# One VectorE scaling per attention step, one head's value sum on GpSimd, the outputs' split one step later, and output products spread over steps 10 to 15

## The chip, the core and the metric

The kernel runs on one core of a Trainium2 chip. The core has five engines that work side by side: TensorE (PE in the profile; its weight loads are PEld), VectorE (DVE), ScalarE (ACT), GpSimd (POOL) and SyncE (SP), which here only issues DMAs. The metric is the device time of one execution in microseconds (us). Three runs of the kernel before gave 1141.34, 1141.52 and 1141.9 us; the median is 1141.52.

## The reference

A two-layer decoder trunk over 512 tokens of width 1024. Layer 0 mixes tokens by chunked spatial gating, layer 1 by sliding-window attention; each is followed by a gated feed-forward block with a causal convolution and by a gated per-layer embedding. The change lies in the attention of layer 1, which is cut here to what is computed:

```python
q = (xn @ w_q).reshape(B, nb, BLOCK, N_KV_HEADS, GQA_GROUP, HEAD_DIM)      # 4 blocks of 128, 4 groups of 4 heads
scores = jnp.einsum('bnikgd,bnjkd->bnkgij', q, kblk) * (HEAD_DIM ** -0.5)  # previous and own block
scores = scores - slopes * dist;  scores = jnp.where(valid, scores, -jnp.inf)
m = jnp.maximum(jnp.max(scores, axis=-1, keepdims=True), sink)
e = jnp.exp(scores - m)
probs = e / (jnp.sum(e, axis=-1, keepdims=True) + jnp.exp(sink - m))
out = jnp.einsum('bnkgij,bnjkd->bnikgd', probs, vblk)
h = h + out.reshape(B, S, N_Q_HEADS * HEAD_DIM) @ w_o
```

A window of 128 keys over blocks of 128 means that each query has exactly one valid key at each of 128 places, either in its own block or in the one before.

## The kernel before

Activations are kept transposed: eight tiles of 128 features by 512 tokens. To keep float32 precision, each operand of a product is split into a high and a low half (`split`: ScalarE casts the high half, VectorE subtracts to get the low one), and a product is three matmuls: high by high, low by high, high by low (`mm3`, lines 181 to 183). Weights come by DMA into raw tiles (`load`, line 129, on SP's queue), are split in units of 1024 columns (`pump`, lines 154 and 155; four units are held) and are handed out by `chunk`. `more` splits one unit ahead of its use. `pieces` lists the weights in the order of their loads.

The attention runs as 16 steps, one per pair of a group g (four heads) and a block n of 128 queries. Step i does:

- `scores(i)`: eight score matmuls into two PSUM tiles (`sc`), for each head by the high and low half of the keys; VectorE picks for each place the own or the previous block's key (line 784), then adds the distance term and finds the minimum (line 788); ScalarE takes the exponential and its sum (line 793). The result `pr` has two buffers. GpSimd puts the sink into an extra column (line 774).
- `weights(i)`: VectorE takes the reciprocal of the four sums (line 801); the four heads' probabilities are scaled one by one, the first by VectorE (line 807), the other three by ScalarE (line 805).
- `turn(i)`: four transposes by TensorE into one PSUM tile (`tr`, line 822), then a split into halves (lines 252 and 253). For n > 0 GpSimd makes masked copies `u` of both halves (line 830).
- `mix(i)`: two or four matmuls with the values (`pv`, line 844) into one PSUM tile whose upper 64 rows are the contribution of the values' low halves. ScalarE copies those rows down (line 848, `side`), VectorE adds them for one head of each pair at a time (line 852, two instructions). Then the sums are split into the outputs' halves: ScalarE casts `oh` (line 856), GpSimd subtracts for `ol` (line 857), two instructions each.

In the program, step i holds `scores(i)`, other products (`fill(i)`), `mix(i - 2)`, `turn(i - 1)` and `weights(i)`. The parts `scores`, `turn` and `weights` stand under `tc.high_priority()`. The order of instructions on each engine is made by the framework's planner: it takes the instructions whose operands it reckons to be ready by priority, and the priority is the place in the program, with the high-priority ones ahead. An engine then works its queue strictly in order, and waits at an instruction whose operands are late.

`fill(i)` takes its work from the table `beside`. Steps 0 to 9 hold the query projections of the next groups (`project`, twelve matmuls a step from step 2 on), and from step 10 on the output product. `merge(m, k0, k1)` adds for output tile m the slices k0 to k1 of its eight, three matmuls each (L181 to L183 with the name `o`); slices 2g and 2g + 1 need the outputs of group g for all four blocks. A tile m keeps its PSUM bank from its first slice to its last. Slices that are not done in the loop are done behind it, followed by the residual's addition (line 885) and the next norm.

PSUM has eight banks, and every tile of it here takes one. The single raw weight tile that the loop uses (`state["tags"] = [0]`) holds one piece of 2048 columns at a time.

Of the kernel before, what the change touches and what calls it, by code (L numbers as in the profile page):

```python
# [13 lines left out]
P = 128  # L14
# [34 lines left out]
def tile_yoco(ctx: ExitStack, tc: tile.TileContext, t, out: bass.AP, out_b: bass.AP):  # L49
# [58 lines left out]
    plan_cols(t["w_kv"][1:2], 1, KD)  # L108
    plan_cols(t["w_q"][1:4], 3, KD)
    plan_cols(t["w_o"], 4, KD)  # L110
    plan_ffn(1)
# [7 lines left out]
    raws, ready = {}, {}  # L119
    state = {"raw": 0, "unit": 0, "next": 0, "tags": [0, 1, 2], "turn": 0, "pt": 0}  # L120

    def load(upto, queue=nc.sync):
        while state["raw"] < min(upto, len(pieces)):
            j = state["raw"]
            a, m = pieces[j][:2]
            tags = state["tags"]
            r = wp.tile([P, 2 * UNIT], F32, tag=f"r{tags[state['turn'] % len(tags)]}", bufs=1, name=f"wraw{j}")
            state["turn"] += 1
            queue.dma_start(r[:, :m].rearrange("p (c m) -> p c m", c=2) if j in paired else r[:, :m], a)
            raws[j] = r  # L130
            state["raw"] += 1
# [119 lines left out]
    def split(src, hi, lo):  # L251
        nc.scalar.copy(hi, src)  # L252
        nc.vector.tensor_sub(lo, src, hi.bitcast(F32))

    def xtiles(pool, pre, tags):
# [385 lines left out]
    def queries(ps, g, j):  # L641
# [17 lines left out]
        for e, q in enumerate(res):  # L659
            me, it = sides[e], sides[1 - e]  # L660
            nc.sync.dma_start(q[me, :].bitcast(F32), hi[me, :])
            nc.sync.dma_start(q[it, :].bitcast(F32), qf[me, :])
        return res
# [65 lines left out]
    def more():  # L729
# [67 lines left out]
    def weights(i):  # L797

        pr, sm = live[i]
        ds = at.tile([P, GQ], F32, tag="ds", bufs=2, name=f"ds{i}")  # L800
        nc.vector.reciprocal(ds, sm)
        for e in range(GQ):
            a, r = pr[:, e, :P], ds[:, e : e + 1]
            if e:
                nc.scalar.activation(a, a, AF.Copy, scale=r)
            else:
                nc.vector.tensor_scalar_mul(a, a, r)
        live[i] = pr
# [7 lines left out]
    def turn(i):  # L816
# [6 lines left out]
        ph, pl = pair(f"p{i}")  # L823
        split(tr, ph, pl)
        live[i] = [(ph, pl)]
# [9 lines left out]
    def mix(i):  # L835
# [14 lines left out]
        a, low = (x.rearrange("p (b e t) -> p e b t", b=2, e=2) for x in (ps[sides[0], :], low))  # L850
        for e in range(2):
            nc.vector.tensor_add(o[sides[e]], a[:, e], low[:, e])
        cols = slice(n * P, (n + 1) * P)
        for b in range(2):
            oh, ol = o2[2 * g + b]
            nc.scalar.copy(oh[:, cols], o[:, b, :])
            (nc.vector if i == last - 1 else nc.gpsimd).tensor_sub(ol[:, cols], o[:, b, :], oh[:, cols].bitcast(F32))
# [252 lines left out]
```

## Time and profile before

| | us |
|---|---|
| median of three runs | 1141.52 |
| the profiled execution's own time | 1141.22 |
| its span, first to last instruction | 1139.5 |
| PE busy | 1127.0 |
| DVE busy | 749.6 |
| ACT busy | 530.0 |
| POOL busy | 107.7 |

A row of instructions gives: line, engine, operation, out<-in by the program's names, shapes, the count; then busy us, mean ns of one, and the idle time before with what ended it. A row of the order of time begins with start and duration in us, and ends, where the engine idled, with how long and for whom. A row of waits reads: engine and line that waited <- what released it: us in total, times, longest. Matmuls are pipelined, so one is shown for longer than the distance to the start of the next.

### The profile page before, as it was taken

The numbers are of one execution on the slowest core, as the hardware profiler recorded it, in microseconds if no ns is written. First come the engines' busy times: TensorE is split into PE (matmuls) and PEld (weight loads), VectorE is DVE, ScalarE is ACT, GpSimd is POOL, SyncE is SP. The second block draws the span as 40 slices with busy tenths as digits, with TensorE's granted clock in tenths as the row PEclk, the third lists the DMA queues.
The fourth block names the chain that finished last, engine by engine and source line by source line (L and its number), as shares of the span: only waits on it lengthen the run. The fifth ranks groups of instructions, "written<-read, shape, count | busy, mean of one in ns | idle before, by whom it ended". The sixth has DMA issues, their size and how long they took to land.

```text
span 1139.5 us, 13604 instructions
## 1 busy us (share of the span) xinstructions
PE 1127.0 (99%) x5266; PEld 940.5 (83%) x5266; DVE 749.6 (66%) x1158; ACT 530.0 (47%) x875; POOL 107.7 (9%) x175
## 2 busy tenths in 40 slices
PE   9999999999999999999999999999999999999997
PEld 7888888888888888888898878888888888888896
DVE  7366477763677367557988977777636763675675
ACT  6533344441344234445657985444313432355562
POOL 2000200000000000021213343000000000000222
PEclk9999999999999999999999999999999999999999
DMA  8422323223223322432224315223223233224302
GB/s 298 145 83 74 111 75 111 101 85 111 78 98 102 111 76 86 134 107 79 74 75 129 93 38 185 98 88 111 78 107 110 66 102 111 93 80 160 111 1 75
DMA packets 25776, 115.41 MB, mean 101 GB/s; under 512 B 2920, under 2 KB 8176, under 8 KB 16240
## 3 DMA queue, kind: packets, MB, share of 16 engines
q1 hardware_dynamic: 25152, 113.89, 29.8%
q8 instruction: 41, 0.67, 0.2%
q10 hardware_dynamic: 560, 0.66, 0.2%
q14 instruction: 23, 0.19, 0.1%
HBM read 108.24 MB, written 2.11 MB: 97 GB/s over the span
## 4 chain that ended last, share of the span: by engine, by line
PE 95%; DVE 2%; issue 1%; ACT 1%; DMA 1%; POOL 0%; SPq 0%; POOLq 0%; DVEq 0%; ACTq 0%
PE up L181 14%; PE up L183 14%; PE up L182 14%; PE d L183 8%; PE d L181 8%; PE d L182 8%; PE gate L181 2%; PE gate L183 2%; PE gate L182 2%; PE u L182 1%; PE u L183 1%; PE u L181 1%; PE o L182 1%; PE o L181 1%; PE o L183 1%; PE q L181 1%
## 5 line engine op out<-in xcount | busy, mean ns | idle before, releaser
L154 ACT CAST wh<-wraw 128x1024 fp32r<-128x1024 f32 (+2 forms) x197 | 202.0, 1028 | 264.6 <-PE d L182 131.0
L155 DVE TENSOR_TENSOR wl<-wraw,wh 128x1024 fp32r<-128x1024 f32 (+1 forms) x198 | 238.4, 1205 | 127.9 <-ACT wh L154 127.6
L181 PE MATMUL up<-nf00h,wh 128*128 128x512 f32 x352 | 137.1, 390 | 0.0
L181 PE MATMUL up<-nf10h,wh 128*128 128x512 f32 x352 | 137.0, 389 | 0.0
L182 PE MATMUL up<-nf00l,wh 128*128 128x512 f32 x352 | 136.9, 389 | 0.0
L183 PE MATMUL up<-nf00h,wl 128*128 128x512 f32 x352 | 136.9, 389 | 0.0
L183 PE MATMUL up<-nf10h,wl 128*128 128x512 f32 x352 | 136.9, 389 | 0.0
L182 PE MATMUL up<-nf10l,wh 128*128 128x512 f32 x352 | 136.9, 389 | 0.0
L181 PE MATMUL d<-ah,wh 128*128 128x512 f32 x352 | 136.9, 389 | 0.0
L182 PE MATMUL d<-al,wh 128*128 128x512 f32 x352 | 136.9, 389 | 0.0
L183 PE MATMUL d<-ah,wl 128*128 128x512 f32 x352 | 136.9, 389 | 0.0
L379 ACT ACTIVATE c<-hs,vec 128x512 f32<-128x512 f32 x88 | 71.5, 815 | 72.0 <-DVE hs L375 71.2
L380 DVE SCALAR_TENSOR_TENSOR c<-hs,vec,c 128x511 f32<-128x511 f32 x88 | 65.8, 749 | 34.5 <-ACT c L379 34.4
L355 DVE TENSOR_TENSOR h<-h,d 128x512 f32<-128x512 f32 x56 | 38.4, 686 | 73.8 <-PE d L183 73.8
L252 ACT CAST ah<-a 128x512 fp32r<-128x512 f32 x44 | 27.4, 622 | 109.5 <-DVE a L385 109.4
L183 PEld LDWEIGHTS up<-nf10h,wl 128*128 128x128 f32 x352 | 66.1, 188 | 13.8
L182 PEld LDWEIGHTS d<-al,wh 128*128 128x128 f32 x352 | 66.1, 188 | 13.8
L183 PEld LDWEIGHTS up<-nf00h,wl 128*128 128x128 f32 x352 | 66.1, 188 | 13.8
L183 PEld LDWEIGHTS d<-ah,wl 128*128 128x128 f32 x352 | 66.1, 188 | 13.7
L182 PEld LDWEIGHTS up<-nf00l,wh 128*128 128x128 f32 x352 | 66.1, 188 | 13.7
L182 PEld LDWEIGHTS up<-nf10l,wh 128*128 128x128 f32 x352 | 66.1, 188 | 13.7
L181 PEld LDWEIGHTS d<-ah,wh 128*128 128x128 f32 x352 | 66.1, 188 | 13.6
(454 smaller groups left out, 2061.7 us busy)
## 6 DMA issues: line engine op xcount, KB each, us to landing
wraw<-in_w_up SPq DMA_DIRECT2D x44, 1024.0 KB, 4.8
wraw<-in_w_down SPq DMA_DIRECT2D x16, 896.0 KB, 4.6
wraw<-in_w_down SPq DMA_DIRECT2D x8, 1024.0 KB, 4.8
wraw<-in_w_gate SPq DMA_DIRECT2D x8, 1024.0 KB, 4.8
wraw<-in_w_u SPq DMA_DIRECT2D x4, 1024.0 KB, 5.9
wraw<-in_w_out SPq DMA_DIRECT2D x4, 1024.0 KB, 4.8
wraw<-in_w_q SPq DMA_DIRECT2D x4, 1024.0 KB, 4.9
wraw<-in_w_o SPq DMA_DIRECT2D x4, 1024.0 KB, 4.9
```

Source lines behind the costliest of these rows:

```text
L154: nc.scalar.copy(hi, src)
L155: nc.vector.tensor_sub(low, src, hi.bitcast(F32))
L181: nc.tensor.matmul(ps, wh[:, a:b], xh, start=st, stop=False)
L182: nc.tensor.matmul(ps, wh[:, a:b], xl, start=False, stop=False)
L183: nc.tensor.matmul(ps, wl[:, a:b], xh, start=False, stop=en)
L252: nc.scalar.copy(hi, src)
L355: nc.vector.tensor_add(h[m], h[m], ps)
L379: nc.scalar.activation(c, hs, AF.Identity, bias=v("conv_b", l * 2 * NJ + col), scale=cw[2])
L380: nc.vector.scalar_tensor_tensor(c[:, 1:], hs[:, : S - 1], cw[1], c[:, 1:], op0=ALU.mult, op1=ALU.add)
```

## The change

- `weights`: the four scalings become one VectorE product of the 128x4x128 probabilities with the reciprocals, broadcast along the last dimension.
- `mix`: ScalarE copies the first head's rows of `pv` (lower 64 rows, 256 columns) into the tile `side` as well; GpSimd adds the first head's two parts from there; VectorE adds the second head's.
- The split of the outputs becomes a function of its own, `finish`. Up to step 13 `finish(i - 3)` follows `turn(i - 1)`, so an output is split a step later than before; from step 14 on it stands ahead of `fill(i)`. The last two outputs are split right behind their `mix`. For the first eleven an order edge (no wait) puts the cast `oh` behind the latest `split` of transposes on ScalarE.
- The table `beside` has the output products of steps 10 to 17 in another order: four tiles m are begun in steps 10 and 11 with the slices of group 0, those of group 1 follow in steps 12 to 14, those of group 2 in steps 14 and 15. Step 12 has a `more`.
- `queries` and `load`: an order edge puts the load of an output weight piece behind the copies of the queries of one group on SP's queue.

```diff
 def load(upto, queue=nc.sync):
...
-            queue.dma_start(r[:, :m].rearrange("p (c m) -> p c m", c=2) if j in paired else r[:, :m], a)
+            ins = queue.dma_start(r[:, :m].rearrange("p (c m) -> p c m", c=2) if j in paired else r[:, :m], a)
+            for front in state["sent"].pop(j, []):
+                behind(ins, front)
...
 def queries(ps, g, j):
...
+            if g > 1 and j:
+                state["sent"].setdefault(outs + g - 1, []).extend(sent)
...
-        10: [(merge, 0, 0, 3), (more,)],
-        11: [(merge, 0, 3, 4), (merge, 1, 0, 2), (more,)],
-        12: [(merge, 1, 2, 4), (merge, 2, 0, 1)],
-        13: [(merge, 2, 1, 4)],
-        14: [(merge, 0, 4, 6), (merge, 1, 4, 6)],
-        15: [(merge, 2, 4, 6)],
-        16: [(merge, 3, 0, 6)],
-        17: [(merge, 4, 0, 6)],
+        10: [(merge, 0, 0, 2), (merge, 1, 0, 2), (more,)],
+        11: [(merge, 2, 0, 2), (merge, 3, 0, 2), (more,)],
+        12: [(merge, 0, 2, 4), (merge, 1, 2, 4), (more,)],
+        13: [(merge, 2, 2, 4), (merge, 3, 2, 3)],
+        14: [(merge, 3, 3, 4), (merge, 0, 4, 6), (merge, 1, 4, 6)],
+        15: [(merge, 2, 4, 6), (merge, 3, 4, 6)],
+        16: [(merge, 4, 0, 6)],
+        17: [(merge, 5, 0, 6)],
...
 def weights(i):
-        for e in range(GQ):
-            a, r = pr[:, e, :P], ds[:, e : e + 1]
-            if e:
-                nc.scalar.activation(a, a, AF.Copy, scale=r)
-            else:
-                nc.vector.tensor_scalar_mul(a, a, r)
+        a = pr[:, :, :P]
+        nc.vector.tensor_mul(a, a, ds.rearrange("p (e o) -> p e o", o=1).to_broadcast([P, GQ, P]))
...
 def mix(i):
...
-        for e in range(2):
-            nc.vector.tensor_add(o[sides[e]], a[:, e], low[:, e])
+        own_a = side[sides[0], 3 * S + i % 2 * N : 3 * S + (i % 2 + 1) * N].rearrange("p (b t) -> p b t", b=2)
+        nc.scalar.copy(own_a, a[:, 0])
+        nc.vector.tensor_add(o[sides[1]], a[:, 1], low[:, 1])
+        nc.gpsimd.tensor_add(o[sides[0]], own_a, low[:, 0])
+        live[i] = o
+
+    def finish(i):
+        g, n = steps[i]
+        o = live.pop(i)
         cols = slice(n * P, (n + 1) * P)
         for b in range(2):
             oh, ol = o2[2 * g + b]
-            nc.scalar.copy(oh[:, cols], o[:, b, :])
+            ins = nc.scalar.copy(oh[:, cols], o[:, b, :])
+            if i + 3 < LATE:
+                behind(ins, state["split"])
             (nc.vector if i == last - 1 else nc.gpsimd).tensor_sub(ol[:, cols], o[:, b, :], oh[:, cols].bitcast(F32))
...
+    LATE = last - 2
...
+        if LATE <= i < last + 1:
+            finish(i - 3)
         if i <= last:
             fill(i)
         if i >= 2:
             mix(i - 2)
+        if i - 2 >= last - 2:
+            finish(i - 2)
...
+        if 3 <= i < LATE:
+            finish(i - 3)
```

More of the change, by code (lines that the diff above doesn't have):

```diff
@@ L109, in tile_yoco @@
     plan_cols(t["w_q"][1:4], 3, KD)
+    outs = len(pieces)
     plan_cols(t["w_o"], 4, KD)
@@ L119, in tile_yoco, with behind @@
     raws, ready = {}, {}
-    state = {"raw": 0, "unit": 0, "next": 0, "tags": [0, 1, 2], "turn": 0, "pt": 0}
+    state = {"raw": 0, "unit": 0, "next": 0, "tags": [0, 1, 2], "turn": 0, "pt": 0, "split": None, "sent": {}}
+    def behind(ins, front):
+        tc.add_manual_dep(ins.ins, front.ins.name,
+                          mybir.DependencyInfo(mybir.DependencyClass.NoSync, mybir.DependencyReason.DATA),
+                          reason="order")
     def load(upto, queue=nc.sync):
@@ L251, in split @@
     def split(src, hi, lo):
-        nc.scalar.copy(hi, src)
+        ins = nc.scalar.copy(hi, src)
         nc.vector.tensor_sub(lo, src, hi.bitcast(F32))
+        return ins
     def xtiles(pool, pre, tags):
@@ L660, in queries @@
             me, it = sides[e], sides[1 - e]
[L661 to L662 removed]
+            sent = [nc.sync.dma_start(q[me, :].bitcast(F32), hi[me, :]),
+                    nc.sync.dma_start(q[it, :].bitcast(F32), qf[me, :])]
+            if g > 1 and j:
+                state["sent"].setdefault(outs + g - 1, []).extend(sent)
         return res
@@ L823, in turn @@
         ph, pl = pair(f"p{i}")
-        split(tr, ph, pl)
+        state["split"] = split(tr, ph, pl)
         live[i] = [(ph, pl)]
```

## The prediction

> **What bounds the kernel now.** I read the page first, then the busy time by stretches, the waits, and the order of time around them.
>
> ```profile
> span 1139.5 us, 13604 instructions
> PE 1127.0 (99%) x5266; PEld 940.5 (83%) x5266; DVE 749.6 (66%) x1158; ACT 530.0 (47%) x875; POOL 107.7 (9%) x175
> ```
> ```profile
> 25.00:591.00 566.00, 566.00 (x2565) 470.79 (x2564) 360.39 (x469) 242.03 (x322) 33.60 (x28) 1.00 0.29 97
> 591.00:645.00 54.00, 54.00 (x308) 46.84 (x307) 44.73 (x145) 45.33 (x141) 20.47 (x54) 1.00 0.42 125
> 645.00:687.00 42.00, 38.33 (x196) 29.85 (x195) 33.33 (x114) 34.74 (x117) 19.50 (x39) 1.00 0.18 56
> 687.00:1132.00 445.00, 445.00 (x2114) 374.66 (x2112) 288.47 (x387) 189.10 (x268) 29.25 (x27) 1.00 0.29 98
> ```
>
> The columns after the length are PE, PEld, DVE, ACT, POOL busy, then granted clock, DMA share and GB/s. TensorE is the bound, at full clock, and it idles in one place that the change can reach: 645 to 687 us, attention steps 10 to 17. Steps 0 to 9 (591 to 645) are full.
>
> ```profile
> 646.60 0.27 PE L822 MATMUL tr<-ident,prs 128*128 128x128 f32 x1
> 646.63 0.36 PE L781 MATMUL sc<-kh,q 128*128 128x256 f32 x1
> 646.83 0.28 PE L782 MATMUL sc<-kl,q 128*128 128x256 f32 x1
> 646.95 0.28 PE L781 MATMUL sc<-kh,q 128*128 128x256 f32 x1
> 649.27 0.39 PE L183 MATMUL o<-oh,wl 128*128 128x512 f32 x1
> 649.50 0.39 PE L844 MATMUL pv<-pts,vt 128*128 128x512 f32 x1
> 662.11 0.50 PE L182 MATMUL o<-ol,wh 128*128 128x512 f32 x1 [0.71 <-POOL ol L857]
> ```
> ```profile
> L781 PE MATMUL sc<-kh,q 128*128 128x256 f32 (+1 forms) x24 | 7.1, 318 | 0.0
> L782 PE MATMUL sc<-kl,q 128*128 128x256 f32 (+1 forms) x24 | 6.5, 291 | 0.0
> L822 PE MATMUL tr<-ident,prs 128*128 128x128 f32 x32 | 6.3, 277 | 2.3 <-DVE prs L807 1.7 <-DVE pts L253 0.5
> ```
> ```profile
> PE tr L822 <- DVE prs L807: 1.7, 3, 0.8
> PE o L182 <- POOL ol L857: 0.7, 1, 0.7
> PE tr L822 <- DVE pts L253: 0.5, 1, 0.5
> PE pv L844 <- ACT prs L793: 0.4, 1, 0.4
> PE o L181 <- ACT oh L856: 0.3, 1, 0.3
> ```
>
> Matmuls overlap, so what counts is the distance of their starts: 0.23 us for 512 columns (649.27 to 649.50), 0.12 for a score product (646.83 to 646.95), and 0.23 for a transpose with a score product (646.60 to 646.83), so 0.11 for the transpose. The 196 matmuls of that stretch are 48 scores, 32 transposes and 116 wide ones: 48 x 0.12 + 32 x 0.11 + 116 x 0.23 = 36.0 us of 42.0. So 6.0 us are lost, the most that this change can win, and the rows of waits name 3.6 of them. A shown gap of 0.47 to 0.80 costs 0.16 more than it shows, as a wide matmul shows 0.39 and starts the next after 0.23.
>
> **The change part by part.** The rows that carry prices:
>
> ```profile
> L805 ACT ACTIVATE prs<-prs,ds 128x128 f32<-128x128 f32 x48 | 15.9, 395 | 0.0
> L430 ACT COPY pef<-pinf 128x256 f32<-128x256 f32 x8 | 2.9, 374 | 1.1 <-PE pinf L183 0.9
> L807 DVE TENSOR_SCALAR prs<-prs,ds 128x128 f32<-128x128 f32 x16 | 6.5, 409 | 0.2
> L852 DVE TENSOR_TENSOR side<-pv,side 64x256 f32<-64x256 f32 x32 | 13.3, 416 | 3.8 <-ACT side L848 3.4
> L335 DVE TENSOR_TENSOR nf1dh<-ident,nf1rh 128x512 fp32r<-128x512 f32 x1 | 0.7, 690 | 0.0
> L857 POOL TENSOR_TENSOR ol<-side,oh 128x128 fp32r<-128x128 f32 x30 | 14.1, 490 | 4.3 <-ACT oh L856 4.2
> L912 POOL TENSOR_TENSOR facc<-facc,fsq 128x256 f32<-128x256 f32 x6 | 4.7, 787 | 5.3 <-ACT fsq L907 5.3
> L282 POOL TENSOR_TENSOR nf1acc<-nf1acc,nf1sq 128x512 f32<-128x512 f32 x5 | 7.5, 1507 | 6.5 <-ACT nf1sq L277 6.4
> ```
> ```profile
> 650.00:655.00 5.00, 3.83 (x22) 3.07 (x23) 4.73 (x21) 4.93 (x18) 1.86 (x5) 1.00 0.47 105
> ```
>
> One scaling. Per step ScalarE loses three of L805 (busy 15.9 us over 16 steps, 0.99 a step), VectorE loses L807 (0.41) and gains a product of 512 columns with one operand broadcast, as L335 has: 0.69. No PE time by itself; the transposes then wait for one instruction, not for four on two engines.
>
> The value sum. VectorE loses one L852 (0.42). ScalarE gains a copy of 64x256 out of PSUM, for which L430 is nearest (same columns, same source): 0.37. GpSimd gains an addition of 64x256: between L857 (128 columns, 0.49) and L282 (512, 1.51), taken as L912 (256), 0.79. Together a step is lighter by 0.62 us on ScalarE and by 0.14 on VectorE, and heavier by 0.79 on GpSimd. The addition waits for both of ScalarE's copies; behind it in GpSimd's queue stand the next step's masks and the subtractions, which PE's value and output products read (a rival below). GpSimd was busy 20.47 of 54 and 19.50 of 42 us. ScalarE is full where PE begins to idle (4.93 of 5.00 in 650 to 655), so its 0.62 is what counts.
>
> The split a step later. The two casts (L856) and two subtractions (L857) stay, but are issued after the next step's work, and order edges put the casts behind the cast of the following transposes on ScalarE: behind them queue only low halves, which the products need two steps on. The same edges hold a load of output weights behind query copies on SP's queue, which is the order that it has already:
>
> ```profile
> 631.71 1.10 SPq L662 DMA_DIRECT2D q<-qf  x2
> 633.39 0.33 SPq L129 DMA_DIRECT2D wraw<-in_w_o  x1
> 682.43 1.22 DVE L155 TENSOR_TENSOR wl<-wraw,wh 128x1024 fp32r<-128x1024 f32 x1 [2.07 <-ACT wh L154]
> ```
>
> so nothing. The third `more` draws a weight split (1.22 on VectorE, seen late at 682.43) forward into steps 12 to 14: VectorE has 42.00 - 33.33 = 8.67 us free there; without that cover it costs 1.2 us once.
>
> Output products. Steps 10 to 15 held 3+3+3+3+4+2 = 18 slices of three matmuls; now 4+4+4+3+5+4 = 24. The six more are 18 x 0.23 = 4.1 us that left the row behind the loop, so PE's sum of work is unchanged, and each step has 9 to 15 independent matmuls where it had 6 to 12; the query steps 2 to 9 had 12 and no idle. What this does to each wait: the three on L807 lose 0.8, 0.5 and 0.5, with 0.16 each: 2.2; each step now has 3 x 0.23 = 0.69 more to run, so of 0.94, 0.60 and 0.60 at most 0.25 stays: 2.0 won (between 0, if the work is put elsewhere, and 2.2). The wait for POOL ol (662.11) is a product that needs the second group's outputs; these slices move from steps 10 and 11 to step 12: 0.9 won (0 to 0.9). The wait on L253, 0.5 + 0.16, is covered as those above: 0.6 won. The waits on ScalarE (0.4 + 0.3, and 0.3 for the two tails) are at step 14, where products need the third group's outputs, whose way grows by GpSimd's 0.79 less ScalarE's backlog of 0.62 a step: 0.7 won (from a loss of 0.8 to a gain of 1.0). Sum 2.0 + 0.9 + 0.6 + 0.7 = 4.2 us. The other 1.8 of the 6.0 are small starts that no row names, taken as staying. What is late next is the third group's output at step 14.
>
> The profiled execution took 1141.22 us round a span of 1139.5, so 1137.0 there; the median of the runs is 0.3 above it, 1141.52: I forecast 1137.3 us.
>
> **The rivals.**
>
> ```profile
> 656.66 0.40 PE L844 MATMUL pv<-u9l,diff 128*128 128x512 f32 x1
> 664.01 0.87 DVE L852 TENSOR_TENSOR side<-pv,side 64x256 f32<-64x256 f32 x2
> ```
>
> First, PSUM, on the other side. From step 11 on four product accumulators are open, where there were three from step 12. Four banks of eight are left for the four tiles of a step (two scores, transposes, values), so each must come free within a step, 8 x 0.12 + 4 x 0.11 + (4 + 12) x 0.23 = 5.1 us. Before, step 9's values were summed at 656.66 and their bank was read to the end only at 664.4: 7.4 us after the start of the last matmul (664.01 is the first of two, 0.4 each). Unchanged but for the 0.4 of the addition and the 0.4 of a scaling in front of it, it is 6.6: 1.5 us late in each of steps 11 to 15, 7.5 lost, 4.2 won: 1144.8. It decides from a lag of 5.9 (0.84 x 5 = 4.2). For it: that lag, and steps 12 to 15 had five banks. Against it: the copy waited on ScalarE behind work that is now removed or put later, so I expect under 5.
>
> ```profile
> 633.68 0.27 DVE L807 TENSOR_SCALAR prs<-prs,ds 128x128 f32<-128x128 f32 x1
> 654.25 0.54 DVE L807 TENSOR_SCALAR prs<-prs,ds 128x128 f32<-128x128 f32 x1
> ```
> ```profile
> 654.07 0.64 POOL L830 TENSOR_SCALAR_AFFINE_SELECT u9l<-pts 128x512 fp32r<-128x512 f32 x1
> 646.42 0.64 POOL L830 TENSOR_SCALAR_AFFINE_SELECT u7l<-pts 128x512 fp32r<-128x512 f32 x1
> ```
> ```profile
> 647.89 0.39 PE L844 MATMUL pv<-u7l,diff 128*128 128x512 f32 x1
> ```
>
> Second, GpSimd becomes late. It also makes the masked copies (L830) that the value products read: u7l ended at 647.06 and was read at 647.89, 0.83 us of slack. The new addition in front, 0.79, and 0.27 for contention with VectorE (the scaling took 0.54 beside u9l and 0.27 alone) make 1.06, so 0.23 late in each of twelve masked steps: 2.8 of the 4.2 is given back, 1140.1. Against it: GpSimd is under half busy, and the masks have priority in the program. The Trainium skill's page "SBUF — State Buffer", section "Who interferes with whom", makes this a lock: a VectorE instruction with two SBUF inputs and a GpSimd one that reads SBUF exclude each other for the whole instruction. The 0.54 beside u9l agrees with such a block; by that rule the new scaling, with its two SBUF inputs, could wait a mask's full 0.64 us.
>
> Third, the change does not reach the waits on outputs, and the added slices alone work: 2.0 won, 1139.5.
>
> **How the numbers follow.** The forecast has 0.55, the PSUM rival 0.20, GpSimd 0.12, the slices alone 0.13. The forecast's own range is 1135.5 (all 6.0 us) to 1138.5 (3.0 won). What a measurement can tell from no change is 0.2%, 2.3 us: faster means under 1139.2. That has the forecast and 0.08 of the last two together, as both lie near the line: 0.63. Within 0.2% has their other 0.17 less 0.02 for worse ends: 0.15. Slower has the PSUM rival with those 0.02: 0.22. The range for 8 in 10 goes from all recovered, 1135.2 with the runs' own 0.3, to the PSUM rival's 1144.8.
>
> **What would show it.** Right: in the stretch from step 10 to the last value product PE idles under 2 us by its waits; no wait of PE on the scaling; ScalarE without 5 us at 4.9; VectorE's scaling near 0.69; steps 0 to 9 still full. The PSUM rival would show as score products or transposes that wait for L852 or the new copy, GpSimd's as value products that wait for L830. Wrong would be new idle time in steps 2 to 9, where VectorE was busy 44.73 of 54 us, or a sum lag that stays near 7 us.

## The result and the profile after

The changed kernel is slower: 1144.11 us, median of seven runs (1143.67 to 1145.44), against 1141.34 us of seven runs of the kernel before beside them (1140.64 to 1141.9). The ratio is 1.0027, 95% interval 1.0016 to 1.0038. The forecast was 1137.3. The profiled execution took 1145.29 us, one of the longer ones; why the runs lie 1.8 us apart is told with the clock below. Line numbers are now those of the changed kernel (scores L793 and L794, transposes L830, their split L261 and L262, values L852, ScalarE's two copies L856 and L860, the additions L861 on VectorE and L862 on GpSimd, output products L190 to L192).

The head of the page and the busy time by stretches, columns as in the prediction:

```profile
span 1143.6 us, 13592 instructions
PE 1129.7 (99%) x5266; PEld 942.5 (82%) x5266; DVE 750.5 (66%) x1142; ACT 521.3 (46%) x843; POOL 124.5 (11%) x191
...
591.00:645.00 54.00, 54.00 (x309) 46.85 (x308) 47.40 (x143) 40.06 (x122) 28.84 (x63) 1.00 0.43 125
645.00:687.00 42.00, 38.89 (x198) 31.91 (x196) 29.92 (x99) 28.70 (x97) 23.37 (x41) 0.96 0.20 64
687.00:1132.00 445.00, 443.07 (x2079) 370.92 (x2077) 287.36 (x381) 190.23 (x271) 33.48 (x32) 1.00 0.28 96
```

ScalarE is relieved (28.70 us in steps 10 to 17, 34.74 before), VectorE too (29.92, 33.33 before), and steps 0 to 9 are still full. Two things are new. The granted clock is 0.96 where it was 1.00, and the stretch behind 687 us, in which TensorE never idled before, lacks 1.93 us. TensorE's waits from step 10 to the first feed-forward products:

```profile
PE sc L793 <- DVE p13l L262: 1.9, 1, 1.9
PE nf1ms L312 <- DVE nf1quarter L304: 1.3, 1, 1.3
PE pv L852 <- DVE neg L800: 0.6, 1, 0.6
PE pv L852 <- DVE pts L262: 0.5, 2, 0.3
PE up L191 <- DVE nf10l L258: 0.4, 1, 0.4
PE sc L793 <- DVE side L861: 0.3, 1, 0.3
```

The waits on the scaling and on GpSimd's `ol` are gone, as meant. In their place stand two single waits that the kernel before doesn't have: a score tile at step 15 (1.9 us), and behind the loop the first feed-forward products (0.4 and 1.3 us). Each is followed by a drop of the clock:

```profile
674.00:675.00 1.00, 0.78 (x2) 0.71 (x3) 0.94 (x5) 0.83 (x5) 0.71 (x2) 0.50 1.04 442
675.00:676.00 1.00, 1.00 (x3) 0.67 (x3) 0.94 (x5) 0.85 (x4) 0.66 (x2) 0.50 0.34 139
676.00:677.00 1.00, 1.00 (x6) 0.93 (x5) 0.00 (x0) 0.00 (x0) 0.22 (x1) 0.50 0.00 0
...
722.00:723.00 1.00, 1.00 (x4) 0.81 (x3) 0.21 (x2) 0.00 (x0) 0.73 (x1) 0.50 0.00 0
723.00:724.00 1.00, 1.00 (x3) 0.74 (x3) 1.00 (x3) 0.00 (x0) 0.00 (x0) 0.50 0.00 0
724.00:725.00 1.00, 1.00 (x4) 0.77 (x3) 0.34 (x1) 0.00 (x0) 0.00 (x0) 0.50 0.00 0
```

At 0.50 a wide matmul starts 0.43 us after the one before it, not 0.23; behind the loop seven matmuls do so in full and two in part, 1.6 us in all.

**The first loss, step 15.** TensorE's, VectorE's and ScalarE's order of time around it:

```profile
670.73 0.28 PE L794 MATMUL sc<-kl,q 128*128 128x256 f32 x1
672.87 0.36 PE L793 MATMUL sc<-kh,q 128*128 128x256 f32 x1 [1.86 <-DVE p13l L262]
```
```profile
670.07 1.22 DVE L164 TENSOR_TENSOR wl<-wraw,wh 128x1024 fp32r<-128x1024 f32 x1
671.21 0.42 DVE L796 COPY_PREDICATED sc<-own,sc 128x256 f32<-128x256 int32 x1
671.97 0.18 DVE L813 RECIPROCAL ds<-sm 128x4 f32<-128x4 f32 x1 [0.33 <-ACT prs L805]
672.06 0.66 DVE L262 TENSOR_TENSOR p13l<-tr,p13h 128x512 fp32r<-128x512 f32 x1
...
674.45 0.42 DVE L861 TENSOR_TENSOR side<-pv,side 64x256 f32<-64x256 f32 x1
```
```profile
668.23 0.58 ACT L856 COPY side<-pv 64x512 f32<-64x512 f32 x1 [0.30 <-PE pv L852]
668.72 1.04 ACT L163 CAST wh<-wraw 128x1024 fp32r<-128x1024 f32 x1
...
671.84 0.35 ACT L860 COPY side<-pv 64x256 f32<-64x256 f32 x1
```

A score tile reads nothing of step 13's transposes, whose split (`p13l`) it waited for; what it needs is their bank. Counted from the first matmul into each tile to its last read, all eight banks were taken at that moment: four open output tiles, the first score tile of step 15, the transposes of step 13, and the values of steps 11 and 12. The bank of step 11's values, summed from 665.6 us on, was read for the last time by the addition at 674.45: ScalarE's second copy for it (671.84) came behind a weight cast (668.72), and VectorE's addition behind the same weight's subtraction (670.07).

**The second loss, behind the loop.** The last output product starts at 712.71 us; in the kernel before it was

```profile
712.46 0.39 PE L183 MATMUL o<-oh,wl 128*128 128x512 f32 x1
```

so with all work up to there the same, the loop has won and lost in equal parts, to 0.25 us. The other 3.9 of the 4.1 us between the two spans come behind it, where VectorE adds the finished output tile to h (L910), splits the normalised h for the feed-forward (`nf10l`, L258) and splits weights (L164), while GpSimd adds up the squares (L292):

```profile
704.08 1.21 DVE L164 TENSOR_TENSOR wl<-wraw,wh 128x1024 fp32r<-128x1024 f32 x1
705.22 3.49 DVE L258 SCALAR_TENSOR_TENSOR nf10l<-h,vec,nf10h 128x512 fp32r<-128x512 f32 x2
708.63 2.31 DVE L164 TENSOR_TENSOR wl<-wraw,wh 128x1024 fp32r<-128x1024 f32 x1
710.86 0.74 DVE L258 SCALAR_TENSOR_TENSOR nf10l<-h,vec,nf10h 128x512 fp32r<-128x512 f32 x1
711.52 0.67 DVE L910 TENSOR_TENSOR h<-h,o 128x512 f32<-128x512 f32 x1
...
715.92 0.67 DVE L910 TENSOR_TENSOR h<-h,o 128x512 f32<-128x512 f32 x1
```
```profile
704.39 5.47 POOL L292 TENSOR_TENSOR nf1acc<-nf1acc,nf1sq 128x512 f32<-128x512 f32 x3 [0.86 <-ACT nf1sq L287]
```

The last addition to h comes 3.0 us after its product was done (712.71 + 0.23); before, VectorE sat waiting for it (`[0.63 <-PE o L183]`, at 712.88). Beside GpSimd's block of 5.47 us, two `nf10l` took 3.49 us, where one alone takes 0.74, and a weight split 2.31 instead of 1.21. The first of these is not new. In the kernel before, two `nf10l` take as long beside a block of two additions; only the slow weight split beside the third addition is added:

```profile
700.29 3.49 DVE L249 SCALAR_TENSOR_TENSOR nf10l<-h,vec,nf10h 128x512 fp32r<-128x512 f32 x2
703.70 1.21 DVE L155 TENSOR_TENSOR wl<-wraw,wh 128x1024 fp32r<-128x1024 f32 x1
```
```profile
700.06 3.17 POOL L282 TENSOR_TENSOR nf1acc<-nf1acc,nf1sq 128x512 f32<-128x512 f32 x2 [0.87 <-ACT nf1sq L277]
```

### The profile page after: what moved, and what is told of

It is laid out like the page before. It is cut to its first block, busy times and chain, and to the rows that moved or that the text cites. A ratio compares the mean times of both kernels' runs of the same rounds, so it can differ in the third digit from the quotient of the medians.

```text
span 1143.6 us, 13592 instructions
## 1 busy us (share of the span) xinstructions
PE 1129.7 (99%) x5266; PEld 942.5 (82%) x5266; DVE 750.5 (66%) x1142; ACT 521.3 (46%) x843; POOL 124.5 (11%) x191
## 4 chain that ended last, share of the span: by engine, by line
PE 93%; DVE 4%; issue 1%; ACT 1%; DMA 0%; POOL 0%; SPq 0%; POOLq 0%; DVEq 0%
PE up L190 14%; PE up L191 14%; PE up L192 14%; PE d L190 8%; PE d L192 8%; PE d L191 8%; PE gate L190 2%; PE gate L191 2%; PE gate L192 2%; PE q L190 1%; PE q L192 1%; PE q L191 1%; PE u L191 1%; PE u L192 1%; PE u L190 1%
## 5 line engine op out<-in xcount | busy, mean ns | idle before, releaser
L164 DVE TENSOR_TENSOR wl<-wraw,wh 128x1024 fp32r<-128x1024 f32 (+1 forms) x198 | 239.2, 1209 | 126.4 <-ACT wh L163 126.1
L190 PE MATMUL up<-nf10h,wh 128*128 128x512 f32 x352 | 137.7, 391 | 0.0
L192 PE MATMUL up<-nf10h,wl 128*128 128x512 f32 x352 | 137.5, 391 | 0.0
L190 PE MATMUL up<-nf00h,wh 128*128 128x512 f32 x352 | 137.1, 390 | 0.0
L192 PE MATMUL up<-nf00h,wl 128*128 128x512 f32 x352 | 136.9, 389 | 0.0
L190 PE MATMUL d<-ah,wh 128*128 128x512 f32 x352 | 136.9, 389 | 0.0
L192 PE MATMUL d<-ah,wl 128*128 128x512 f32 x352 | 136.9, 389 | 0.0
L192 PEld LDWEIGHTS up<-nf10h,wl 128*128 128x128 f32 x352 | 66.5, 189 | 13.9
L190 PEld LDWEIGHTS up<-nf10h,wh 128*128 128x128 f32 x352 | 66.5, 189 | 13.9
L192 PEld LDWEIGHTS d<-ah,wl 128*128 128x128 f32 x352 | 66.1, 188 | 13.7
L190 PEld LDWEIGHTS d<-ah,wh 128*128 128x128 f32 x352 | 66.1, 188 | 13.7
L192 PEld LDWEIGHTS up<-nf00h,wl 128*128 128x128 f32 x352 | 66.1, 188 | 13.6
```

Source lines behind the costliest of these rows:

```text
L164: nc.vector.tensor_sub(low, src, hi.bitcast(F32))
L190: nc.tensor.matmul(ps, wh[:, a:b], xh, start=st, stop=False)
L192: nc.tensor.matmul(ps, wl[:, a:b], xh, start=False, stop=en)
```

## The experiments

All times are medians; the kernel before ran beside each and took 1141.2 to 1141.5 us.

### The table of output products alone, and fewer open tiles

Two theories stood at first: A, that the six slices drawn into the loop are missing as cover behind it; B, that banks at step 15 eat the gain; and as their rival C, that the new instructions themselves cost the time. The first run has the kernel before with the new rows 10 to 17 of `beside` (the diff of the table, shown with the change) and nothing else.

> The kernel before with the changed kernel's table of output products alone (24 slices in steps 10 to 15, four open tiles, the third weight split); scaling, value sum and outputs' split as before. Theory A, the tail: the six slices that left the row of products behind the loop were the cover under which VectorE worked off the norm's splits, and without them TensorE idles and falls to half clock at the first feed-forward products, 3.4 us between 700 and 1100 us in the changed kernel. It expects the same loss here, less the 1.5 to 2.5 us that the added fill wins in steps 11 to 14: 1142.2 to 1143.5 us. Theory B, the banks: the loss is the 1.9 us stall of the second score tile of step 15 and the half clock behind it, with the copy of own_a and the later value sum as its cause; here neither is there, so the added slices alone win 1.5 to 2.5 us: 1138.8 to 1139.8 us. Theory C, the other parts (one scaling, GpSimd's add, the later split) cost the time: at most 1141.3 us.

It took 1145.13 us (ratio 1.0035, 1.0022 to 1.0049), more than any of the three expected, with the same two clock drops as the changed kernel (0.97 from 645 to 700 us, 0.96 from 700 to 740) and the same two waits at the head of TensorE's list:

```profile
PE sc L781 <- DVE p13l L253: 2.2, 1, 2.2
PE nf1ms L302 <- DVE nf1quarter L294: 1.3, 1, 1.3
```

So C falls: the table alone makes the loss. B's cause as I had put it falls too, since neither ScalarE's second copy nor GpSimd's addition is in this kernel, and the stall is. A and B are not alternatives: each loss is there. The waits on the scaling and on GpSimd's `ol` are gone in this kernel too, so the table alone is enough to remove them.

The next run keeps the other parts of the change and gives the table three open tiles until step 15 and before's 18 and 34 slices.

```diff
-        10: [(merge, 0, 0, 2), (merge, 1, 0, 2), (more,)],
-        11: [(merge, 2, 0, 2), (merge, 3, 0, 2), (more,)],
-        12: [(merge, 0, 2, 4), (merge, 1, 2, 4), (more,)],
...
-        16: [(merge, 4, 0, 6)],
-        17: [(merge, 5, 0, 6)],
+        10: [(merge, 0, 0, 2), (merge, 1, 0, 1), (more,)],
+        11: [(merge, 1, 1, 2), (merge, 2, 0, 2), (more,)],
+        12: [(merge, 0, 2, 4), (merge, 1, 2, 3)],
...
+        16: [(merge, 3, 0, 6)],
+        17: [(merge, 4, 0, 6)],
```

> The changed kernel with a table that opens three output tiles instead of four until step 15, adds 18 slices in steps 10 to 15 and leaves 34 behind the loop as before, without the third weight split. Theory A: with the six slices back behind the loop the 3.4 us there go, while the loop keeps what the other parts won: 1139.0 to 1141.0 us; TensorE waits for nothing between 700 and 740 us. Theory B: one bank fewer is held open and the weight split ahead of step 13's transposes is gone, so the stall of step 15 goes (3.5 us with its half clock), and the tail's loss stays at 3.4 us: 1140.0 to 1141.5 us by the time, told apart by the tail, where up would still wait for nf10l and run at half clock. Theory C: the other parts stay, so 1144 us stays.

1140.52 us (1140.28 to 1140.97), ratio 0.9994 (0.9985 to 1.0004): both stalls are gone, TensorE is busy 40.00 of 40 us from 700 to 740, and the clock is 1.00 throughout. A and B both expected it; C did not.

### Step 15: what holds the bank

The third `more` was taken out, four tiles still open:

```diff
-        12: [(merge, 0, 2, 4), (merge, 1, 2, 4), (more,)],
+        12: [(merge, 0, 2, 4), (merge, 1, 2, 4)],
```

> The changed kernel without the third weight split at step 12 (one line of the table), everything else as changed. Theory B1, that the split of w_o's weights (1.22 us of VectorE, 1.04 us of ScalarE) ahead of the transposes' split of step 13 makes the bank of step 15 late: TensorE's 1.9 us wait and the half clock behind it go, 1140.7 to 1142.3 us. Theory B2, that the four open tiles and the late value sum do it alone: the wait stays, 1144.1 us within 0.5. Theory A says nothing of step 15, but that the weight split now falls behind the loop, where VectorE is late already: up to 1.2 us more there.

And it was put into the table with three open tiles:

```diff
-        12: [(merge, 0, 2, 4), (merge, 1, 2, 3)],
+        12: [(merge, 0, 2, 4), (merge, 1, 2, 3), (more,)],
```

> The run with three open tiles until step 15 (18 slices in steps 10 to 15, 34 behind the loop), with the third weight split at step 12 put back. Theory B as a sum of two conditions (four banks held by output tiles, and the split in front of step 13's transposes' split): with a fifth bank free the split costs no bank, 1140.3 to 1141.2 us as without it, and the second score tile of step 15 waits under 0.5 us. Theory B1 alone (the split is enough): 1.5 to 3.5 us more than without it, 1142.0 to 1144.0 us.

Without it: 1141.98 us (1140.52 to 1143.13), the wait at step 15 gone. With it and three tiles: 1140.79 us, no wait there either. So, with the other parts as changed, the stall needs both, four open tiles and the third `more`. But not for the reason in the expectation. The run without it has the same weight split at nearly the same time, as VectorE's order of time shows:

```profile
670.02 0.42 DVE L861 TENSOR_TENSOR side<-pv,side 64x256 f32<-64x256 f32 x1
670.47 1.22 DVE L164 TENSOR_TENSOR wl<-wraw,wh 128x1024 fp32r<-128x1024 f32 x1
```

The products draw that split in any case. All that the third `more` does is to put it some places earlier in the program, and with that ahead of the copy and the addition of step 11's value sum: the addition runs at 674.45 with it and at 670.02 without. One place in the order keeps a bank 4.4 us longer.

Moved to step 16 instead, where VectorE has room, it did nothing more than leaving it out:

```diff
-        16: [(merge, 4, 0, 6)],
+        16: [(merge, 4, 0, 6), (more,)],
```

> The changed kernel with the third weight split moved from step 12 to step 16, where VectorE is busy 1.8 of 5 us (675 to 680 us of the run without it); same slices, same splits. Theory A+B1 (the split of w_o's weights at step 12 makes step 15's bank late; the tail is short of cover by VectorE's backlog): the loop's 1.9 us wait is gone as in the run without the split, and the backlog behind the loop is one split of 1.22 to 1.55 us shorter, so of the 2.1 us that TensorE loses at the first feed-forward products 0.5 to 0.9 us stay and the clock stays full: 1138.6 to 1139.6 us. If the split at any place late in the loop costs the same: 1144 us. If the tail's loss has nothing to do with VectorE's backlog: 1140.5 to 1143.1 us, as without the split.

1140.96 us (1140.55 to 1142.76). Step 15 is mended; the tail is not, against the expectation: behind the loop there are six weight splits with and without it, so there was no backlog to shorten.

### The tail: is it cover?

Eighteen useless products ahead of the last output tile:

```diff
+            if m == KD - 1:
+                mm3(psum("cover"), box[3][:6], o2[:6], P)
             merge(m, box.get(f"k{m}", 0), KD)
```

> The changed kernel with eighteen products into a tile that nobody reads, 18 x 0.227 = 4.1 us of TensorE, put ahead of the last output tile behind the loop; they compute nothing that is used. Theory A: TensorE idles behind the loop for want of cover, 3.4 us with the half clock; the useless products fill that time and the time rises by 0.2 to 1.0 us only: 1144.3 to 1145.1 us. If the tail isn't short of cover: the whole 4.1 us more, 1148.2 us.

1145.45 us, a little above the range: 4.1 us of added work cost 1.3 us (1.5 when each is counted from the kernel before beside it), and TensorE waits for nothing from 700 to 740 us (40.00 of 40). The tail is short of cover. Where the cover has to stand was then got wrong. Four slices of step 16 were put behind the last value sum, with no third `more`:

```diff
-        16: [(merge, 4, 0, 6)],
-        17: [(merge, 5, 0, 6)],
+        16: [(merge, 4, 0, 2)],
+        17: [(merge, 4, 2, 6), (merge, 5, 0, 6)],
```

> The changed kernel without the third weight split, and with four of the six slices of step 16 moved behind the last value sum (step 17), so that as many slices as before, 34, cover the tail, while steps 10 to 15 keep their 24. Theory A: the last value sum comes 4 x 0.68 = 2.7 us earlier (step 16's transposes and value sum stand in TensorE's queue behind these slices, not behind VectorE: the last reciprocal is done at 676.4 us, the transposes of its step start at 683.8 us), VectorE's work behind the loop starts as much earlier, and the 2.1 us lost at the first feed-forward products go, with the half clock: 1138.2 to 1139.2 us, and the runs lie within 0.7 us of each other. If instead it is the sum of slices behind the last score product that counts, nothing changes: 1140.5 to 1143.1 us as without the split.

1141.91 us (1140.52 to 1143.12), the same as without that move, and TensorE's longest waits unchanged:

```profile
PE nf1ms L312 <- DVE nf1quarter L304: 1.3, 1, 1.3
PE o L190 <- ACT oh L872: 0.9, 1, 0.9
PE up L191 <- DVE nf10l L258: 0.4, 1, 0.4
```

With the third `more` at step 16 as well,

```diff
-        16: [(merge, 4, 0, 2)],
+        16: [(merge, 4, 0, 2), (more,)],
```

> Both: step 16's slices moved behind the last value sum, and the third weight split at step 16. Theory A: the tail has cover enough already by the moved slices, so the split adds nothing: within 0.4 us of the run with the moved slices alone, 1138.2 to 1139.2 us. If step 16's VectorE is needed for the last step's transposes' split after the slices have moved: up to 1.2 us more.

it took 1141.27 us (1140.84 to 1143.13), with the same waits.

VectorE's norm work begins only when an output tile is finished, and these slices run ahead of the first finished tile. So a whole long tile was left behind the loop again, three in place of two, while steps 10 to 15 keep their 24 slices:

```diff
-        16: [(merge, 4, 0, 6)],
-        17: [(merge, 5, 0, 6)],
+        16: [(merge, 4, 0, 1)],
+        17: [(merge, 4, 1, 6)],
```

> The run without the third weight split, with step 16's and 17's slices cut to six and all eight slices of tile 5 left behind the loop, so that three long tiles end behind the loop as before; steps 10 to 15 keep 24 slices. The earlier run with the moved slices put them ahead of the first finished tile, and TensorE lost the same 2.0 us. Theory A, as that run mends it: VectorE's norm work can begin only when the first tile is finished, so the cover is what TensorE does between the first and the last finished tile: 5 x 1.36 + 3 x 5.44 = 23.1 us before and here, 6 x 1.36 + 2 x 5.44 = 19.0 us in the changed kernel. It expects no wait at the first feed-forward products, no half clock and 1138.3 to 1139.3 us, runs within 0.8 us of each other. If the wait there has another cause than that distance, it stays: 1140.5 to 1143.1 us.

1139.57 us (1139.1 to 1139.82), ratio 0.9984 (0.9974 to 0.9993): faster than both kernels though just above the range, no wait at the first feed-forward products, clock 1.00. Two slices were moved back to step 16:

```diff
-        16: [(merge, 4, 0, 1)],
-        17: [(merge, 4, 1, 6)],
+        16: [(merge, 4, 0, 3)],
+        17: [(merge, 4, 3, 6)],
```

> The best run with two slices of step 17 moved back to step 16, ahead of the last transposes, where TensorE waited 0.84 us for GpSimd's masked weights. If that wait is a want of cover ahead of the last value sum: 0.4 to 0.8 us less, 1138.8 to 1139.2 us. If the two slices are then missing between the last value sum and the first tile behind the loop, where 0.28 us was lost: 1139.6 us or more.

1139.31 us, little changed; the 0.84 us at the last step went and 0.92 us appeared ahead of the first tile, where 0.28 had been (shown as gaps of 0.67, 0.75 and 0.12, with 0.16 each).

### The tail: what needs the cover

Distance between finished tiles explains when the stall comes, not what fills the time. Three runs ask VectorE's queue. The first gave the norm's work the planner's high priority:

```diff
-            nc.vector.tensor_add(h[m], h[m], box[f"o{m}"])
-            nf.take(m)
+            with tc.high_priority():
+                nc.vector.tensor_add(h[m], h[m], box[f"o{m}"])
+                nf.take(m)
```

> The run without the third weight split, with the additions into h and the norm's splits behind the loop put ahead of the weight splits in the order of the queues. Two weight splits stood between the sixth tile and the last addition (2.31 us and 1.55 us of VectorE), which came 2.9 us behind the last product. If it is the order in VectorE's queue that makes the tail late, 1138.4 to 1139.4 us; if VectorE and GpSimd have too much to do in 19.0 us whatever the order (theory A in its strict form), the 2.0 us stay or move to a later weight: 1140.3 to 1143.1 us.

1141.12 us, and 0.4 and 1.5 us of TensorE's time still lost. It tells little: the planner left two weight splits (3.44 us) ahead of the seventh tile's addition and one ahead of the last.

So the order was forced, three weight splits behind the norm's last reduction:

```diff
+    nf.turn()
+    state["late"] = nf.reduced
...
-            nc.vector.tensor_sub(low, src, hi.bitcast(F32))
+            low_ins = nc.vector.tensor_sub(low, src, hi.bitcast(F32))
+            if state.get("late"):
+                if state.get("kept"):
+                    behind(low_ins, state["late"])
+                state["kept"] = True
```

> The run without the third weight split, with three of the six weight splits that VectorE does behind the loop put behind the norm's last reduction in its queue; slices, tiles and GpSimd's additions as there (28 slices behind the loop). Theory A1, the order: two of these splits (2.31 and 1.55 us) stand in front of the last addition, which comes 2.9 us behind its product; with them behind, the addition follows its product, the 2.0 us at the first feed-forward products go: 1138.3 to 1139.3 us, as with the long tile back. Theory A2, GpSimd: nf10l and the remaining split still take twice their time beside GpSimd's additions, and 1.0 us or more of the wait stays: 1139.5 to 1143 us.

1140.63 us (1140.06 to 1141.29). The last addition now follows its product without delay and the wait for `nf10l` is gone, but the one for `nf1quarter` stays at 1.4 us. The reduction came earlier, and the planner put its product earlier too. By the numbers that is theory A2's range, but the order alone was not cleanly tested.

The last one leaves slices, tiles and weight splits alone and takes GpSimd out:

```diff
-            self.square(k, nc.vector if k == KD - 1 else None)
+            self.square(k, nc.vector if k == KD - 1 or self.name == "nf1" else None)
```

> The run without the third weight split, with the sums of squares of the norm behind the loop added by VectorE instead of GpSimd: VectorE gets six additions of 0.68 us, 4.1 us more, and loses what GpSimd's additions cost it, 2 x 1.0 us on nf10l, 1.1 and 0.3 us on two weight splits, 3.4 us. Theory A1: the order stays, so the wait stays or grows by some 0.7 us: 1140.5 to 1144 us. Theory A2: the operations of VectorE are back at 0.75 and 1.21 us and the wait shrinks: 1138.5 to 1139.5 us.

1138.81 us (1138.33 to 1139.49), ratio 0.9976 (0.9967 to 0.9986), the fastest of all, with the changed kernel's 28 slices behind the loop. VectorE does six additions more and is in time; no wait is left there. The eight `nf10l` as groups (least/median/most ns, first and last start), in the changed kernel and in this run:

```profile
L258 DVE SCALAR_TENSOR_TENSOR nf10l<-h,vec,nf10h x8: 739/750/1791, 697.4 to 717.7; 128x512 fp32r<-128x512 f32 x8
```
```profile
L258 DVE SCALAR_TENSOR_TENSOR nf10l<-h,vec,nf10h x8: 746/749/753, 695.5 to 713.2; 128x512 fp32r<-128x512 f32 x8
```

None takes 1.79 us any more. VectorE's order is nearly that of the run without the third split: in both, three weight splits stand between the sixth tile's addition and the last one, and one behind it. So the wait goes without a change of order, as A2 says: GpSimd's additions doubled what VectorE did beside them. From the rows above that is 3.49 - 2 x 0.75 = 2.0 us on two `nf10l` and 1.1 on a weight split. The 2.0 are in the kernel before as well, hidden under its longer cover; the 1.1 came with the third addition in the block, when six short tiles ended 1.36 us apart and not five. With three long tiles left (1139.57 us) the block is two additions and 3.17 us again.

Two controls, the same line in the changed kernel and in the kernel before:

> The changed kernel with one line more: VectorE, not GpSimd, adds the norm's squares behind the loop. Theory A2: the tail's 1.9 us and its half clock (1.5 us) go, the 1.9 us of step 15 and the half clock behind it stay: 1140.5 to 1142.3 us. If the third weight split has used up what VectorE would need: 1144 us.

> The kernel before with the same one line. Theory A2 with the cover as its condition: behind the loop TensorE waits for nothing in the kernel before, so nothing is to be won: 1141.3 us within 0.4. If GpSimd's additions cost time whatever the cover: 1139.0 to 1140.5 us.

The changed kernel with it takes 1141.64 us, and its tail is full; the wait at step 15 and the 0.50 behind it stay. The kernel before with it takes 1141.78 us, 0.3 above the runs beside it, so no gain (1.0003, 0.9994 to 1.0013): there the three long tiles hide what GpSimd costs. These two close the sum: 1144.11 - 1141.64 = 2.5 us is the tail, 1141.64 - 1138.81 = 2.8 us is step 15, and without both the change is worth 1141.34 - 1138.81 = 2.5 us.

### What the other three parts are worth

Each was undone alone, the scaling and the value sum in the run with three open tiles (1140.52 us), the split a step later in the one with three long tiles left (1139.57 us).

```diff
-        a = pr[:, :, :P]
-        nc.vector.tensor_mul(a, a, ds.rearrange("p (e o) -> p e o", o=1).to_broadcast([P, GQ, P]))
+        for e in range(GQ):
+            a, r = pr[:, e, :P], ds[:, e : e + 1]
+            if e:
+                nc.scalar.activation(a, a, AF.Copy, scale=r)
+            else:
+                nc.vector.tensor_scalar_mul(a, a, r)
```

> The run with three open tiles (18 slices in steps 10 to 15), with the scaling done as before: one head by VectorE, three by ScalarE. It tells the price of the one scaling by itself, which the prediction put among the 2.0 us won on the waits for the scaling. If the one scaling pays: TensorE waits for the scaling again, 0.5 to 2.0 us more, 1141.0 to 1142.5 us. If only the place of the slices paid: 1140.5 us within 0.3.

Scaling as before: 1142.17 us, 1.65 more (1.4 when each run is counted from the kernel before beside it). The price was expected, the way to it was not: TensorE doesn't wait for the scaling in this run. Its longest waits are for `ol`, for a masked copy, for the minimum of the scores and for the transposes' split (0.8, 0.7, 0.7 and 0.6 us). These waits come to 2.8 us, against 2.6 in the run with the one scaling, so they don't name where the time goes. ScalarE is busy 37.71 of 42 us in it from 645 to 687 us, against 31.22; that the price is ScalarE's time is likely, but not shown.

```diff
-        nc.scalar.copy(own_a, a[:, 0])
-        nc.vector.tensor_add(o[sides[1]], a[:, 1], low[:, 1])
-        nc.gpsimd.tensor_add(o[sides[0]], own_a, low[:, 0])
+        for e in range(2):
+            nc.vector.tensor_add(o[sides[e]], a[:, e], low[:, e])
```

> The run with three open tiles, with both heads' value sums added by VectorE as before, without ScalarE's copy of the other half and without GpSimd's addition. If GpSimd's part pays (VectorE gets 0.43 us a step, the bank is free after one addition): 0.3 to 1.0 us more, 1140.8 to 1141.5 us. If the copy on ScalarE (0.41 us) costs what VectorE wins: 1140.5 us within 0.3; if it costs more, faster: 1139.8 us.

Value sum by VectorE alone: 1142.57 us, 2.05 more (1.8 counted as above), twice the upper end of what was expected.

```diff
         if i >= 2:
             mix(i - 2)
-        if i - 2 >= last - 2:
             finish(i - 2)
```

(The two other calls of `finish` and the order edge on its cast are gone with it.)

> The best run (three long tiles left behind the loop, no third split) with the outputs' split in the same step as the value sum, as before. If the later split pays what the prediction gave it with the wait on GpSimd's ol and ScalarE's copy (0.9 and 0.7 us): 1140.4 to 1141.3 us. If the wait is only moved: 1139.6 us within 0.3.

Outputs' split in the same step: 1141.88 us, 2.3 more, again more than expected.

All three parts pay, but these prices can't be added: they come to 6.0 us, and the whole change wins 2.5 us with its two losses mended. Each is what is lost when one part is missing from a table that suits all three. With the changed kernel's own table, which stalls, the three together are worth 1.0 us (1145.13 - 1144.11). The order edge on the load of the output weights was not undone alone.

For the added slices the nearest pair is the run with three open tiles (18 slices in steps 10 to 15) and the one with three long tiles left (24), both with 34 slices behind the loop: 1140.52 - 1139.57 = 0.95 us (1.2 counted as above). The two differ in the order of the tiles too.

Without GpSimd's help in the value sum, the wait of step 15 for a bank is there even with three open tiles, at the head of TensorE's waits in that run:

```profile
PE sc L793 <- DVE p13l L262: 1.7, 1, 1.7
PE tr L830 <- DVE prs L815: 1.4, 1, 1.4
```

## Why the prediction was wrong

**The failed step** is the one on the output products: "The six more are 18 x 0.23 = 4.1 us that left the row behind the loop, so PE's sum of work is unchanged". The sum is unchanged, but the row behind the loop was treated as if it hid nothing, and no work was named that it hides. It hid VectorE's norm work, which GpSimd's additions of squares make twice as long in places. Without the six slices between the first and the last finished tile, TensorE waited 1.7 us there and then, in some executions, ran at half clock; the price of this step was 2.5 us (changed kernel with and without GpSimd's additions), not nothing. The rows were in the profile of before: `nf1acc` on GpSimd at 1.5 us each, and beside it two `nf10l` of 3.49 us.

**The third `more`** was the second failure: it "draws a weight split (1.22 on VectorE, seen late at 682.43) forward into steps 12 to 14", and "without that cover it costs 1.2 us once". It drew nothing forward; it moved one weight split ahead of one value sum, and with four tiles open that held the eighth bank. Its price was 2.8 us.

**The PSUM rival** named the right resource and gave it 0.20. Its lag was to decide from 5.9 us. Step 11's values have 674.45 + 0.42 - 667.7 = 7.2 us from their last matmul's start to their last read. It was to strike in each of steps 11 to 15 and struck in one. The lags of steps 9, 10 and 13 are 4.5, 2.4 and 4.5 us; step 12's 6.6 holds the stall itself. In the fastest run step 11 has 2.9 us, under the 5 that were expected. The rival's symptom, a score product that waits, is there for 1.9 us on a tile that only frees the bank, and for 0.3 us on L861, as it had said. Its 1144.8 lies near the result by luck: about half of the loss comes from the tail, of which it says nothing, and its lag of before was 664.4 - 656.66 = 7.7 us, not 7.4, so that its own sum would have given 1.8 us a step, not 1.5.

**The GpSimd rival** looked in the wrong place. In the changed kernel's loop no value product waited for a masked copy (in two other runs one did, for 0.7 us each). The new scaling took 0.69 us in the median and 1.07 at most, so it lost at most 0.38 us to GpSimd, not a mask's full 0.64. The contention that cost time was behind the loop. The Trainium skill's page "SBUF — State Buffer", section "Who interferes with whom", which was weighed for the scaling, says that a VectorE instruction with two inputs in SBUF contends with a GpSimd instruction that reads SBUF. `nf10l` and the weight split have two such inputs, and the trace agrees: 0.74 and 1.21 us alone, 1.74 and 2.31 beside `nf1acc`.

**What was right.** PE's waits on the scaling and on `ol` went, and as the prediction said it is the table that removes them: they are gone with the table alone. But what the parts are worth is not what these waits showed. Undoing the scaling costs 1.65 us and brings no wait on it back; undoing the later split costs 2.3 us, of which one wait on `ol` shows 0.7; the added slices were put at "2.0 won", and the nearest pair of runs gives about 1. Wrong in size: with the two losses mended the change wins 2.5 us, not 4.2. The fastest run still shows 0.9 us for `oh` of the third group at step 14, the term taken as 0.7 won though its range went to a loss of 0.8, and it shows 0.9 us more for the value sums' inputs and banks. The sign that was to show the change right, under 2 us of waits, is met there (1.8 us) and not in the changed kernel (3.3 us).

## What to carry to other kernels

Work moved out of a full stretch may have been the cover of another engine, so name what ran beside it, and measure the cover between the first and the last event that feeds that engine, not as a total. Count PSUM banks by the last read of each tile, and treat a change of place in a queue as a change: with four tiles open, one weight split ahead of one addition cost 2.8 us. Two engines that slow each other cost nothing as long as the engine that bounds the kernel covers them both (no gain from the one line in the kernel before); where the cover is short, giving one of them all of the work can be faster (2.5 us in the changed kernel).

## What the runs showed of the chip that was not expected

About 2 us of idle time was enough for the granted clock to fall to 0.50 for some 3.3 us. It isn't certain: with the same waits behind the loop (0.4 and 1.3 us) the run without the third `more` kept 1.00 in its profile (1140.6 us), and the run with the third `more` at step 16 fell to 0.50 (1142.72 us). The run with the value sum back on VectorE idled 1.7 and 1.4 us within 5 us at a clock of 1.00. The rows at 719 us of the run with the third `more` at step 16:

```profile
719.00:720.00 1.00, 1.00 (x4) 0.75 (x3) 0.09 (x1) 0.00 (x0) 0.83 (x1) 0.50 0.36 148
720.00:721.00 1.00, 1.00 (x4) 0.81 (x3) 0.74 (x3) 0.00 (x0) 0.19 (x1) 0.50 0.00 0
```

That fits the 2 us by which most runs with a stall in the tail spread (1140.5 to 1143.1 us), and by which the run with three long tiles doesn't (1139.1 to 1139.8 us). The clock of whole executions agrees: in the run without the third `more` the five at 1140.5 to 1141.5 us were granted 0.998 or 0.999, the five at 1142.5 to 1143.1 us 0.997 or 0.998; of the changed kernel's executions the three longest 0.996 and the other four 0.997. The run with the forced order, whose one wait there is 1.4 us, has no long executions (1140.1 to 1141.3 us). The Trainium skill's page "TensorE: Matmul & The Clock Gate", Part 1, has the clock halve after an idle window of about 3.4 us and come back after a busy one of that length; the window runs freely. The length of the drop (some 3.3 us) and its chance nature agree; the idle time here was shorter than that window. What decides whether a gap of 2 us brings the drop stays open.
